# Splitting the up-projection weights of three pairs ahead of time and interleaving their products at the seam between output projection and feed-forward

## The chip, the cores and the metric

The kernel runs on one core of a Trainium2 chip as one launch. The metric is the device time of a run in microseconds (us); three runs of the kernel before are shown, and their median counts. The profile is one further execution, taken by the hardware profiler.

## What is computed

One decoder block in float32: 1024 positions and 16 learned ones, model width 1024, feed-forward width 4096. The part that matters here is the end of the layer, word for word:

```python
mix = jax.nn.sigmoid(g_s5) * y_s5 + jax.nn.sigmoid(g_m) * y_m
h = _layer_norm(ALPHA * h + mix @ w_o[layer], ln1_g[layer], ln1_b[layer])
ff = jnp.square(jax.nn.relu(h @ w_up[layer] + b_up[layer])) @ w_down[layer]
h = _layer_norm(ALPHA * h + ff, ln2_g[layer], ln2_b[layer])
```

Ahead of it stand one combined input projection, a state-space mixer (S5) with a gated linear unit, and a matrix-memory mixer (mLSTM); `mix` joins the two.

## The kernel before

Every product is made in float32 precision from pieces: an operand is split into a high part (`hi`, type float32r, an `activation` Copy on ScalarE, ACT) and a low part (`lo`, the difference, a `tensor_tensor` on VectorE, DVE), and `mm3` (lines 208 to 225) issues three matmuls for each term: hi by hi, hi by lo, lo by hi. TensorE (PE) therefore waits for ACT and DVE wherever an operand has just been split.

The work runs in stages. First the layer norm of the input, then a list of jobs (`ORDER`, then the GLU jobs and the jobs `g`/`m` with `ym`), each of which loads a weight tile, splits it, multiplies and evacuates. Beside the jobs run "lanes": generators that issue a few instructions whenever the matmuls issued so far have moved a notional clock past the time that the generator yielded. One of them, `ah_scale` (line 1090), prepares the residual `ALPHA * h` row by row and stores it in DRAM; it is added when the first GLU job begins.

Then comes the seam that the change is about. `wo_mm` (line 1227) multiplies one of eight rows of 128 positions (t = 0 to 7) by `w_o`: two halves of 512 columns, 24 matmuls each, each evacuated on DVE into `ACC[t]` (line 1233). `ln1_norm` (line 1235) takes the statistics (DVE `bn_stats` on both halves, `bn_aggr`, a square root on ACT, a reciprocal and three Newton steps on DVE) and normalises the row; `ln1_tr` (line 1241) transposes it on PE (8 transposes), scales it on ACT and DVE into `hf`, and splits part of it into `h1h` and `h1l`.

The up product of the feed-forward follows. `w_up` is taken in 16 pairs of column blocks, and each pair is multiplied by a scheme of seven products (numbers 1 to 7, `BLKS`) of 12 matmuls each in place of eight. Products 1, 2 and 3 use `h1h`/`h1l` (`H1`); products 4 to 7 use sums of the row blocks made by `h1_sums` (four DVE instructions for each of four column groups c = 0 to 3) and split by `h1_split` into `th`/`tl` (`T[n]`, one ACT and one DVE instruction for each c). Products 1 and 2 need only the rows t = 0 to 3. Each pair's weights are likewise summed (`up_sums`, four DVE instructions) and split (`split_to`, lines 1305 to 1308, into `wuh`/`wul`) while the pair ahead is multiplied; products of one pair accumulate on each other in PSUM, so that product 2 waits until ACT has copied the result of product 1 out (line 1361), and product 7 until DVE has added product 6 (line 1367).

At the seam the first two pairs are loaded early (`up_load`), products 1 and 2 of pairs 0 and 1 stand around the last transposes, and everything else that they need is summed and split there and then. The order of instructions on each engine is chosen by a scheduler that simulates the program at build time, except inside `tc.manual_schedule`, where the order of the code is kept. All DMAs are issued on SyncE's queue (SP), in order. Tiles come from pools: `slot` has 30 buffers of a row block, `espot` has four, `mmps` has five PSUM banks, `sdps` three.

Of the kernel before, what the change touches and what calls it, by code (L numbers as in the profile page):

```python
# [108 lines left out]
def decoder_block(  # L109
# [18 lines left out]
    def mmps(name="mm"):  # L128
        return psum.tile([P, 512], F32, tag="mm", bufs=5, name=name)
# [959 lines left out]
    def ah_scale():  # L1089
        gb = [slot("gB0"), slot("bB0")]  # L1090
        for i in range(2):
            nc.sync.dma_start(gb[i][:, :D], row_bcast(ln0r, D, i * D))
        rs = {}
        for t in range(9):
            if t < 8:
                rs[t] = slot("ahr")
                nc.sync.dma_start(rs[t][:, :D], ah0_dr[t * P:(t + 1) * P, :])
            if t == 0:
                yield 4.0
                for i in range(2):  # L1100
                    v_.tensor_scalar(gb[i][:, :D], gb[i][:, :D], ALPHA, None, op0=OP.mult)
                yield 2.0
                continue
            r = rs.pop(t - 1)
            for i, op in enumerate((OP.mult, OP.add)):
                v_.tensor_tensor(r[:, :D], r[:, :D], gb[i][:, :D], op=op)
                yield 4.5
            nc.sync.dma_start(ah_dr[(t - 1) * P:t * P, :], r[:, :D])

    for w in ORDER.split():  # L1110
        n, i = w[0], int(w[1:])
# [56 lines left out]
    for i, j in enumerate(jobs):  # L1168
        if j.raw is None and j.w is None:
            load_w(j)  # L1170
        if j.w is None:
            split_w(j)
        if j.ran:
            next_split(jobs, i)
        for d in (1, 2):
            if i + d < len(jobs) and jobs[i + d].raw is None and jobs[i + d].w is None:
                load_w(jobs[i + d])
        if j.tag == S5_START:
            lanes["s5c"].add(s5_pre())
        if j.tag and j.tag[0] == "o":  # L1180
            while int(j.tag[1:]) not in HMREADY:
                lanes["cv"].drain()
                lanes["ml"].step()
        if j.tag == "glu":
            lanes["ah"].add(ah_scale())
        if j.tag == "hmo":
            for l in lanes.values():
                l.drain()
            mid_ctx.close()
            ring_ctx = ExitStack()  # L1190
            ring[0] = ring_ctx.enter_context(tc.tile_pool(name="ring", bufs=1, side="left"))
# [35 lines left out]
    def wo_mm(t):
        hi, lo = MH.pop(t)
        for c0, c1 in HALF:
            ps = mmps()  # L1230
            mm3(ps, [(hi[:, k * P:(k + 1) * P], lo[:, k * P:(k + 1) * P], wo_hi[:, k, c0:c1], wo_lo[:, k, c0:c1])
                     for k in range(KT)])
            v_.tensor_tensor(ACC[t][:, c0:c1], ps, ACC[t][:, c0:c1], op=OP.add)

    def ln1_norm(t):
        acc = ACC[t]
        mv, y = row_stats(acc, "l1", const)
# [54 lines left out]
    def h1_split(n):  # L1292
        T[n] = (f8("th", F32R), f8("tl", F32R))
        for c in range(4):
            r = {1: RAW[c][:, 0:512], 2: RAW[c + 4][:, 512:1024], 3: RAW[c + 4][:, 0:512], 4: RAW[c][:, 512:1024]}[n]
            r = c3(r)
            a_.activation(c4(T[n][0], c * P), r, AF.Copy)
            v_.tensor_tensor(c4(T[n][1], c * P), r, f32(c4(T[n][0], c * P)), op=OP.subtract)  # L1298

    def up_load(p):  # L1300
        UR[p] = [espot("wur"), espot("wur")] if p < 2 else [slot("wur"), slot("wur")]
# [9 lines left out]

    def up_sums(p):
        r1, r2 = UR[p]
        a11, a12, a21, a22 = r1[:, 0:512], r1[:, 512:1024], r2[:, 0:512], r2[:, 512:1024]
        n1, n2 = slot("wus"), slot("wus")
        v_.tensor_tensor(n1[:, 0:512], a21, a22, op=OP.add)
        v_.tensor_tensor(n1[:, 512:1024], n1[:, 0:512], a11, op=OP.subtract)
        v_.tensor_tensor(a21, a11, a21, op=OP.subtract)
        v_.tensor_tensor(n2[:, 0:512], a12, n1[:, 512:1024], op=OP.subtract)
        UR[p] += [n1, n2]  # L1320
# [33 lines left out]
    def up_step(p, n):  # L1354
# [12 lines left out]
            v_.tensor_tensor(c["e2"][:, 0:512], c["b"], c["p1"], op=OP.add)  # L1367
        elif n == 2:
            up_prod(p, 2, c["a"], False)
            c["x1"] = slot("upx")  # L1370
            x = c["x1"][:, 0:512]
# [208 lines left out]
    mix_split(0)  # L1580
    mix_split(1)
    ah_load(0)
    PRE = 2
    for t in range(8):
        if t + 1 < 8:
            ah_load(t + 1)
        wo_mm(t)
        if t == 0:
            for tt in range(2, 8):
                mix_split(tt)  # L1590
            MIX.clear()
        ln1_norm(t)
        if t > 0:
            ln1_tr(t - 1)
        if t > 4:
            h1_sums(t - 5)
        if t in (5, 6):
            up_load(t - 5)
        if t in (6, 7):
            PREP[1](t - 6)  # L1600
    up_step(0, 1)
    ln1_tr(7)
    up_step(0, 2)
    h8_ctx.close()
    ffn[0] = ctx.enter_context(tc.tile_pool(name="ffn", bufs=1, side="right"))
    h1_sums(3)
    h1_split(2)
    up_step(1, 1)
    up_sums(0)
# [9 lines left out]
    for p in range(NP):
        todo = [n for n in UPO if p >= PRE or n not in (1, 2)]  # L1620
        nxt = []
        if p + 1 < NP:
            nxt = [n for n in range(5) if p + 1 >= PRE or n != 1]
        if PRE <= p + 2 < NP:
# [119 lines left out]
```

## Time and profile before

| | us |
|---|---|
| runs of the kernel before | 1574.76, 1576.25, 1576.30 |
| median | 1576.25 |
| the profiled execution | 1577.17 |
| its span, first to last instruction | 1575.1 |
| PE busy in the span | 1531.5 |
| DVE busy | 1020.1 |
| ACT busy | 592.0 |

The time of an execution is the span and some 2 us around it. A line of a timeline gives the start, the duration, the engine, the source line, the operation with the tile that it writes and the tiles that it reads, and in brackets how long the engine had been idle before it and which engine and line released it. Matmuls are pipelined: the duration shown for one is longer than the distance from its start to the next one's start, and it is that distance which counts.

### The profile page before, as it was taken

What the parts mean: (1) busy time and instruction counts of PE and PEld (TensorE: products, weight loads), DVE (VectorE), ACT (ScalarE), POOL (GpSimd) and SP (SyncE); (2) the same over time, 40 slices, a digit from 0 to 9 for tenths busy, and PEclk for the clock granted to TensorE, in tenths of its full rate; (3) what the DMA queues carried; (4) which work ended last, traced back from release to release, by engine and by line L of the source; (5) the groups of instructions that cost most, each with busy time, mean ns of one, the idle gap of its engine ahead of it and who ended that gap; (6) DMA issues with size and microseconds to landing.
All of it is one profiled execution on the core that took longest, in us unless ns stands there. A gap on an engine that the chain in (4) does not pass through costs nothing.

```text
span 1575.1 us, 20280 instructions
## 1 busy us (share of the span) xinstructions
PE 1531.5 (97%) x7679; PEld 1289.3 (82%) x7679; DVE 1020.1 (65%) x1984; ACT 592.0 (38%) x916; POOL 112.0 (7%) x153
## 2 busy tenths in 40 slices
PE   7899999999999999999999989999999999999997
PEld 7898988998777888878888877888888787888886
DVE  7677555489767725632228687566666579875886
ACT  4433253423354332221115244444444434432440
POOL 3200000254214000000000000000000000000000
PEclk9999999999999999999999999999999999999999
DMA  6301212212332443521124204444443699666742
GB/s 233 123 18 56 85 41 98 82 35 78 105 88 67 131 139 126 193 74 52 43 94 161 81 40 138 133 148 147 151 150 132 199 354 374 204 226 232 237 170 107
DMA packets 99010, 210.50 MB, mean 134 GB/s; under 512 B 15240, under 2 KB 33104, under 8 KB 98912
## 3 DMA queue, kind: packets, MB, share of 16 engines
q1 hardware_dynamic: 98912, 209.21, 39.5%
q8 instruction: 60, 0.98, 0.3%
q14 instruction: 38, 0.31, 0.1%
HBM read 153.40 MB, written 54.60 MB: 132 GB/s over the span
## 4 chain that ended last, share of the span: by engine, by line
PE 88%; DVE 7%; ACT 2%; DMA 2%; issue 1%; SPq 0%; POOLq 0%; ACTq 0%; DVEq 0%
PE mm L223 21%; PE mm L222 21%; PE mm L221 21%; PE sd L222 5%; PE sd L223 5%; PE sd L221 5%; PE mm L217 2%; PE pu L474 1%; PE pn L470 1%; PE pn L471 1%; DMA wiB<-wrow_dr 1%; DVE hf L1039 1%; DVE cy L296 1%; DVE tl L1298 1%; PE pt L510 1%
## 5 line engine op out<-in xcount | busy, mean ns | idle before, releaser
L223 PE MATMUL mm<-hT_hi,wlo 128*128 128x512 f32 (+3 forms) x576 | 216.2, 378 | 5.3 <-DVE wlo L203 5.3
L221 PE MATMUL mm<-hT_hi,whi 128*128 128x512 f32 (+3 forms) x576 | 218.4, 379 | 0.3 <-ACT whi L202 0.3
L222 PE MATMUL mm<-hT_lo,whi 128*128 128x512 f32 (+3 forms) x576 | 216.3, 375 | 0.0
L203 DVE TENSOR_TENSOR wlo<-wraw,whi 128x1024 fp32r<-128x1024 f32 (+1 forms) x58 | 71.8, 1240 | 97.1 <-ACT whi L202 96.8
L223 PEld LDWEIGHTS mm<-hT_hi,wlo 128*128 128x128 f32 x576 | 108.5, 189 | 22.5 <-DVE wlo L203 5.8
L221 PEld LDWEIGHTS mm<-hT_hi,whi 128*128 128x128 f32 x576 | 108.7, 189 | 17.1 <-issue 0.5
L222 PEld LDWEIGHTS mm<-hT_lo,whi 128*128 128x128 f32 x576 | 108.7, 189 | 16.7 <-issue 0.2
L1465 ACT ACTIVATE dwh<-wdr 128x1024 fp32r<-128x1024 f32 x56 | 58.9, 1054 | 97.6 <-DVE wdr L1450 32.6
L202 ACT ACTIVATE whi<-wraw 128x1024 fp32r<-128x1024 f32 (+1 forms) x60 | 62.8, 1053 | 84.0 <-PE mm L222 74.0
L222 PE MATMUL sd<-dwl,dah 128*128 128x512 f32 x240 | 94.4, 393 | 0.0
L223 PE MATMUL sd<-dwh,dal 128*128 128x512 f32 x240 | 94.2, 393 | 0.0
L221 PE MATMUL sd<-dwh,dah 128*128 128x512 f32 x240 | 91.9, 393 | 0.0
L1462 DVE TENSOR_TENSOR dal<-da,dah 128x1024 fp32r<-128x1024 f32 x56 | 68.1, 1218 | 33.9 <-ACT dah L1461 32.8
L221 PE MATMUL mm<-dwh,dah 128*128 128x512 f32 (+1 forms) x224 | 84.1, 378 | 1.3 <-ACT dwh L1465 1.3
L222 PE MATMUL mm<-dwl,dah 128*128 128x512 f32 (+1 forms) x224 | 84.6, 379 | 0.4 <-DVE dwl L1466 0.3
L223 PE MATMUL mm<-dwh,dal 128*128 128x512 f32 (+1 forms) x224 | 84.3, 377 | 0.0
L1461 ACT ACTIVATE dah<-da 128x1024 fp32r<-128x1024 f32 x56 | 58.7, 1051 | 63.3 <-DMA da<-act_dr 33.5
L1308 DVE TENSOR_TENSOR wul<-wus,wuh 128x1024 fp32r<-128x1024 f32 (+1 forms) x32 | 30.6, 957 | 74.4 <-issue 58.0
L1573 POOL TENSOR_TENSOR arow<-arow,b2B 128x256 f32<-128x256 f32 x1 | 1.1, 1088 | 1065.0 <-ACT arow L1572 1065.0
L222 PE MATMUL mm<-tl,wuh 128*128 128x512 f32 x192 | 75.9, 395 | 0.9 <-DVE tl L1298 0.9
L221 PE MATMUL mm<-th,wuh 128*128 128x512 f32 x192 | 75.9, 396 | 0.8 <-DVE upe L1367 0.8
L223 PE MATMUL mm<-th,wul 128*128 128x512 f32 x192 | 76.0, 396 | 0.0
(409 smaller groups left out, 3765.4 us busy)
## 6 DMA issues: line engine op xcount, KB each, us to landing
da<-act_dr SPq DMA_DIRECT2D x56, 512.0 KB, 5.7
wdr<-in_wdn_dram SPq DMA_DIRECT2D x56, 512.0 KB, 6.1
wraw<-in_wf_dram SPq DMA_DIRECT2D x36, 512.0 KB, 4.6
wur<-in_wup_dram SPq DMA_DIRECT2D x32, 512.0 KB, 4.3
act_dr<-upy SPq DMA_DIRECT2D x64, 256.0 KB, 3.0
act_dr<-upx SPq DMA_DIRECT2D x48, 256.0 KB, 2.7
wdr<-in_wdn_dram SPq DMA_DIRECT2D x8, 1024.0 KB, 9.9
hm_dr<-hmF SPq DMA_DIRECT2D x8, 512.0 KB, 3.0
```

The lines of the kernel that those rows point to most:

```text
L202: a_.activation(hi[:, :n], r[:, :n], AF.Copy)
L203: todo.append(lambda e=v_, r=r, hi=hi, lo=lo, n=n: e.tensor_tensor(lo[:, :n], r[:, :n], f32(hi[:, :n]), op=OP.subtract))
L217: t_.matmul(ps, tm[i], tm[j], start=(w == 0 and k == 0), stop=(w == 2 and k == n - 1))
L221: t_.matmul(ps, ah, bh, start=(i == 0 and part[0]), stop=False, skip_group_check=skip)
L222: t_.matmul(ps, ah, bl, start=False, stop=False, skip_group_check=skip)
L223: t_.matmul(ps, al, bh, start=False, stop=(i == n - 1 and part[1]), skip_group_check=skip)
L296: v_.scalar_tensor_tensor(y[:, :LEN], pre[:, w:w + LEN], convt[:, ci, w:w + 1], y[:, :LEN], op0=OP.mult, op1=OP.add)
L470: t_.matmul(pn[:, :257], qi[:, c0:c0 + n], Cs[c][:, :257], start=True, stop=False)
L1308: v_.tensor_tensor(lo[:, :n], raw[:, :n], f32(hi[:, :n]), op=OP.subtract)
L1461: a_.activation(ah[:, :D], a[:, :D], AF.Copy)
L1462: v_.tensor_tensor(alo[:, :D], a[:, :D], f32(ah[:, :D]), op=OP.subtract)
L1465: a_.activation(wh, raw[i], AF.Copy)
```

## The change

Four things are done.

1. The weights of the first three pairs (`PRE = 3`) are loaded, summed and split much earlier, by a new generator `up_early` in the lane of `ah_scale`. For each pair it makes the seven weight blocks as hi and lo beside each other in one tile `wpre` and stores the tile to a DRAM buffer `wu_dr` on SP: 21 stores. `ah_scale` now starts at job `g4`, three jobs ahead of the GLU jobs, and yields 1.5 instead of 4.5, and `up_early` follows it.
2. At the seam these 21 tiles are read back from `wu_dr` by `pre_load`: 128 x 1024 elements each, into the four `espot` buffers, issued on GpSimd's queue (POOL), with a float32 source and a float32r destination. Four loads are issued ahead; after that each product issues the load of the product four places behind it, when it has released its own buffer.
3. The 21 products of the three pairs are interleaved: 1 and 2 of all three pairs first, with the transposes of the last row between, then product 6 of the three pairs, product 7 of the three, then 5, 4 and 3. The order on DVE and PE is that of the code from `ln1_norm(5)` up to product 7 of the third pair (`tc.manual_schedule` for these two engines); ACT, SP and POOL keep the scheduler's order. The statistics of a half row are taken right behind its evacuation, and the transposes of rows 5 and 6 stand between the halves of rows 6 and 7.
4. The tile `x1` of a pair is dropped; its two results are written into the halves of `e1`.

The diff, cut to its core:

```diff
@@ up_early, a new generator behind ah_scale (whose yield goes from 4.5 to 1.5)
+    wu_dr = dram.tile([PRE, 7, P, 1024], F32, name="wu_dr")
+    def up_early():
+        for p in range(PRE):
+            r = [slot("wur"), slot("wur")]
+            for j in range(2):
+                nc.sync.dma_start(r[j][:, :D], wup[2 * p + j].rearrange("p k f -> p (k f)"))
+            yield 3.0
+            a11, a12, a21, a22 = r[0][:, 0:512], r[0][:, 512:1024], r[1][:, 0:512], r[1][:, 512:1024]
+            n1, n2 = wsums(a11, a12, a21, a22)
+            yield 3.0
+            for n, w in ((1, a11), (2, a12), (3, n2[:, 0:512]), (4, a22), (5, n1[:, 0:512]), (6, n1[:, 512:1024]),
+                         (7, a21)):
+                o = slot("wpre", F32R)
+                a_.activation(o[:, 0:512], w, AF.Copy)
+                v_.tensor_tensor(o[:, 512:1024], w, f32(o[:, 0:512]), op=OP.subtract)
+                nc.sync.dma_start(wu_dr[p, n - 1], f32(o[:, 0:1024]))
+                yield 0.9
@@ where the lanes are fed
-        if j.tag == "glu":
+        if j.tag == "g4":
             lanes["ah"].add(ah_scale())
+            lanes["ah"].add(up_early())
@@ the loads at the seam
+    def pre_load(p, n):
+        w = espot("wpre", F32R)
+        g_.dma_start(w, wu_dr[p, n - 1])
+        UW[p, BLKS[n][0]] = (w[:, 0:512], w[:, 512:1024])
@@ the seam (before: one loop over the eight rows, then the pairs one by one)
+    todo = [(0, 1), (1, 1), (0, 2), (2, 1), (1, 2), (2, 2)] + [(p, n) for n in (6, 7, 5, 4, 3) for p in range(PRE)]
+    loads = iter(todo)
+    def pre(p, n):
+        up_step(p, n)
+        ld = next(loads, None)
+        if ld:
+            pre_load(*ld)
+    for _ in range(4):
+        pre_load(*next(loads))
+    with tc.manual_schedule(engines={mybir.EngineType.DVE, mybir.EngineType.PE}):
+        ln1_norm(5)
+        wo_row(6, lambda: (ln1_tr(5), h1_sums(0)))
+        ln1_norm(6)
+        h1_sums(1)
+        wo_row(7, lambda: (ln1_tr(6), h1_sums(2)))
+        ln1_norm(7)
+        h8_ctx.close()
+        ffn[0] = ctx.enter_context(tc.tile_pool(name="ffn", bufs=1, side="right"))
+        h1_split(2, range(3))
+        for i in range(6):
+            pre(*todo[i])
+            if i == 2:
+                ln1_tr(7)
+                h1_sums(3)
+                h1_split(2, (3,))
+        h1_split(3)
+        for n, nt in ((6, 1), (7, 4)):
+            for p in range(PRE):
+                pre(p, n)
+                if p == 1:
+                    h1_split(nt, range(2))
+                if p == 2:
+                    h1_split(nt, range(2, 4))
```

What the change does to the order on PE at the seam: before, behind the last matmul of row 7, with what each matmul waits for (`h1h`, `h1l`, `th`, `tl` are the activations, `wuh`, `wul` the weights split at the seam, `ident` marks transposes):

```order
L221 MATMUL mm_8355<-h1h_7733,wuh_8254 128x512 [waits Activation_49]
L223 MATMUL mm_8355<-h1h_7733,wul_8255 128x512 [waits DVE_49]
...
L1252 MATMUL ln1_8325<-ident_74,acc_8052 128x128 [waits DVE_49]
...
L221 MATMUL mm_8427<-h1h_7733,wuh_8351 128x512 [waits Activation_49]
...
L221 MATMUL mm_8355<-h1h_7737,wuh_8254 128x512 [waits Activation_49]
...
L1252 MATMUL ln1_8371<-ident_74,acc_8155 128x128 [waits DVE_49]
...
L221 MATMUL mm_8427<-h1h_7737,wuh_8351 128x512 [waits Activation_49]
...
L222 MATMUL sd_8548<-tl_8479,wuh_8448 128x512 [waits DVE_49]
```

And on PE in the changed kernel, from the first product to the first one that uses the sums (`wpre` are the tiles read back, `DMASW` the semaphores of POOL's loads):

```order
L222 MATMUL mm_8493<-h1h_7848,wpre_8253 128x512 [waits DMASW1_49]
...
L222 MATMUL mm_8476<-h1h_7852,wpre_8255 128x512 [waits DMASW2_49,Activation_49]
...
L1290 MATMUL ln1_8528<-ident_74,acc_8272 128x128 [waits DVE_49]
...
L222 MATMUL mm_8556<-h1h_7848,wpre_8257 128x512 [waits DMASW3_49]
...
L222 MATMUL mm_8493<-h1h_7852,wpre_8491 128x512 [waits DMASW4_49,Activation_49]
...
L222 MATMUL mm_8556<-h1h_7852,wpre_8508 128x512 [waits DMASW5_49,Activation_49]
...
L223 MATMUL mm_8617<-tl_8469,wpre_8525 128x512 [waits DVE_49]
```

The transposes of row 6 have moved ahead of these products (between the halves of row 7), row 7's stand behind three products, no product waits for a weight split on ACT or DVE, and each waits for a load instead.

On DVE, before, from the last evacuation of row 7 on (`L1298` splits `tl`, `L1308` splits weights, `L1233` to `L180` and `L169` to `L172` are row 7's evacuation, statistics and Newton steps, `L1259`, `L1269` and `L1287` to `L1290` belong to row 6):

```order
L1233 TENSOR_TENSOR acc<-mm,acc 128x512
L1298 TENSOR_TENSOR tl<-hf,th 128x4x128
L179 BN_STATS l1st<-acc 128x6
L1298 TENSOR_TENSOR tl<-hf,th 128x4x128 x2
L180 BN_AGGR l1mv<-l1st 128x2
L1298 TENSOR_TENSOR tl<-hf,th 128x4x128 x5
L1259 TENSOR_SCALAR hf<-ln_8325,ln1t 128x128 x2
L1308 TENSOR_TENSOR wul<-wur,wuh 128x1024
L169 RECIPROCAL l1y<-l1y 128x1
...
L170 SCALAR_TENSOR_TENSOR l1u<-l1mv,l1y 128x1
```

And in the changed kernel, from the same evacuation on:

```order
L1264 TENSOR_TENSOR acc<-mm,acc 128x512
L1269 BN_STATS l1st<-acc 128x6
L1274 BN_AGGR l1mv<-l1st 128x2
L170 RECIPROCAL l1y<-l1y 128x1
L171 SCALAR_TENSOR_TENSOR l1u<-l1mv,l1y 128x1
L172 SCALAR_TENSOR_TENSOR l1u<-l1u,l1y 128x1
L173 SCALAR_TENSOR_TENSOR l1y<-l1u,l1y 128x1
L1276 TENSOR_SCALAR acc<-acc,l1mv,l1y 128x1024
L1337 TENSOR_TENSOR tl<-hf,th 128x4x128 x3
```

Row 7's normalisation is now one unbroken run, with the splits of `tl` behind it and no weight split near it.

POOL's queue had no DMA before. In the changed kernel it holds, behind its last work for S5, four loads and then 17 that each wait for PE:

```order
L1346 DMA wpre_8253<-wu_dr_102 128x1024
L1346 DMA wpre_8255<-wu_dr_102 128x1024
L1346 DMA wpre_8257<-wu_dr_102 128x1024
L1346 DMA wpre_8491<-wu_dr_102 128x1024 [waits DMASW0_49,PE_49]
L1346 DMA wpre_8508<-wu_dr_102 128x1024 [waits DMASW1_49,PE_49]
```

What moved here is the delivery of weights: from SP and a split on ACT and DVE to one load on POOL for each product.

## Rows read from the trace of the kernel before

**Rows 1.** The page: its head, and busy time of each engine with its share of the span.

```profile
span 1575.1 us, 20280 instructions
...
PE 1531.5 (97%) x7679; PEld 1289.3 (82%) x7679; DVE 1020.1 (65%) x1984; ACT 592.0 (38%) x916; POOL 112.0 (7%) x153
```

**Rows 2.** Who waited for whom, PE alone, whole span: us in total, times, longest. The first row is the opening layer norm; the other five all lie between 919 and 985 us.

```profile
PE ln L1029 <- DVE x L1022: 11.5, 8, 2.0
PE mm L221 <- ACT wuh L1307: 2.4, 1, 2.4
PE mm L221 <- ACT upe L1361: 2.2, 2, 1.5
PE sd L222 <- DVE tl L1298: 2.1, 1, 2.1
PE mm L222 <- DVE tl L1298: 0.9, 1, 0.9
PE mm L221 <- DVE upe L1367: 0.8, 1, 0.8
```

**Rows 3.** Busy time by stretch at the seam: us of PE, PE weight loads, DVE, ACT and POOL with their instructions in brackets, then the granted PE clock, the DMA share and GB/s.

```profile
925.00:950.00 25.00, 18.43 (x78) 13.82 (x77) 23.02 (x47) 17.23 (x35) 0.00 (x0) 0.93 0.13 53
935.00:940.00 5.00, 5.00 (x18) 3.96 (x17) 5.00 (x14) 2.31 (x4) 0.00 (x0) 0.75 0.00 0
950.00:975.00 25.00, 23.34 (x99) 18.09 (x98) 18.62 (x27) 10.97 (x16) 0.00 (x0) 1.00 0.34 116
```

**Rows 4.** Timeline of PE at the seam, from the first up product on, and two rows out of a steady stretch, 11 matmuls apart.

```profile
926.78 0.40 PE L221 MATMUL mm<-h1h,wuh 128*128 128x512 f32 x1
...
929.55 1.03 PE L1252 MATMUL ln<-ident,acc 128*128 128x128 f32 x8
932.95 0.50 PE L221 MATMUL mm<-h1h,wuh 128*128 128x512 f32 x1 [2.36 <-ACT wuh L1307]
...
935.75 0.63 PE L221 MATMUL mm<-h1h,wuh 128*128 128x512 f32 x1
936.18 0.63 PE L222 MATMUL mm<-h1l,wuh 128*128 128x512 f32 x1
...
943.58 0.50 PE L221 MATMUL mm<-h1h,wuh 128*128 128x512 f32 x1 [1.53 <-ACT upe L1361]
...
949.12 0.50 PE L222 MATMUL sd<-tl,wuh 128*128 128x512 f32 x1 [2.06 <-DVE tl L1298]
...
953.12 0.50 PE L222 MATMUL mm<-tl,wuh 128*128 128x512 f32 x1 [0.88 <-DVE tl L1298]
...
956.74 0.50 PE L221 MATMUL mm<-th,wuh 128*128 128x512 f32 x1 [0.78 <-DVE upe L1367]
...
997.35 0.39 PE L222 MATMUL mm<-tl,wuh 128*128 128x512 f32 x1
...
999.91 0.39 PE L221 MATMUL mm<-th,wuh 128*128 128x512 f32 x1
```

**Rows 5.** Timeline of DVE and ACT: row 7's evacuation, the end of its statistics, its square root, reciprocal and normalisation.

```profile
926.98 0.69 DVE L1233 TENSOR_TENSOR acc<-mm,acc 128x512 f32<-128x512 f32 x1 [2.19 <-PE mm L223]
...
930.05 0.20 DVE L180 BATCH_NORM_AGGREGATE l1mv<-l1st 128x2 f32<-128x12 f32 x1
...
932.79 0.29 ACT L168 ACTIVATE l1y<-l1mv,eps_t 128x1 f32<-128x1 f32 x1
...
934.91 0.15 DVE L169 RECIPROCAL l1y<-l1y 128x1 f32<-128x1 f32 x1
...
940.09 0.81 DVE L1238 TENSOR_SCALAR acc<-acc,l1mv,l1y 128x1024 f32<-128x1024 f32 x1
```

**Rows 6.** Busy time by stretch, columns as in rows 3: from the first up product to the end of PE's last wait.

```profile
926.70:957.00 30.30, 22.07 (x91) 16.11 (x90) 28.27 (x54) 19.97 (x39) 0.00 (x0) 0.94 0.20 72
```

**Rows 7.** Groups of instructions by line and shape: the splits of up weights. Busy us, mean ns of one, idle time before.

```profile
L1308 DVE TENSOR_TENSOR wul<-wur,wuh 128x1024 fp32r<-128x1024 f32 x32 | 38.9, 1215 | 0.8 <-ACT wuh L1307 0.8
...
L1308 DVE TENSOR_TENSOR wul<-wus,wuh 128x512 fp32r<-128x512 f32 x16 | 11.0, 690 | 71.5 <-issue 58.0 <-PE mm L222 11.2 <-PE sd L222 2.3
...
L1307 ACT ACTIVATE wuh<-wus 128x512 fp32r<-128x512 f32 x16 | 10.1, 631 | 24.9 <-DVE wul L1308 24.9
```

**Rows 8.** Busy time by stretch, columns as in rows 3: the GLU jobs.

```profile
575.00:600.00 25.00, 25.00 (x109) 20.27 (x108) 14.63 (x17) 7.08 (x9) 0.00 (x0) 1.00 0.32 112
600.00:625.00 25.00, 25.00 (x109) 20.26 (x108) 12.35 (x15) 5.84 (x8) 0.00 (x0) 1.00 0.48 166
625.00:650.00 25.00, 25.00 (x111) 20.30 (x109) 14.69 (x16) 4.89 (x7) 0.00 (x0) 1.00 0.37 131
650.00:675.00 25.00, 25.00 (x109) 20.27 (x108) 16.03 (x18) 9.09 (x11) 0.00 (x0) 1.00 0.69 235
```

**Rows 9.** DMA issues by line: count, KB each, median us from issue to landing. All of them stand on SP's queue.

```profile
wur<-in_wup_dram SPq DMA_DIRECT2D x32, 512.0 KB, 4.3
...
wdr<-in_wdn_dram SPq DMA_DIRECT2D x8, 1024.0 KB, 9.9
...
ah_dr<-ahr SPq DMA_DIRECT2D x8, 512.0 KB, 3.0
...
arow<-res_dr SPq DMA_DIRECT2D x8, 512.0 KB, 11.8
```

More of the change, by code (lines that the diff above doesn't have):

```diff
@@ L43 @@
 NM = 1
+PRE = 3
 ZD = 1
@@ L1106, in ah_scale, with wsums @@
                 v_.tensor_tensor(r[:, :D], r[:, :D], gb[i][:, :D], op=op)
-                yield 4.5
+                yield 1.5
             nc.sync.dma_start(ah_dr[(t - 1) * P:t * P, :], r[:, :D])
+    wu_dr = dram.tile([PRE, 7, P, 1024], F32, name="wu_dr")
+    def wsums(a11, a12, a21, a22):
+        n1, n2 = slot("wus"), slot("wus")
+        v_.tensor_tensor(n1[:, 0:512], a21, a22, op=OP.add)
+        v_.tensor_tensor(n1[:, 512:1024], n1[:, 0:512], a11, op=OP.subtract)
+        v_.tensor_tensor(a21, a11, a21, op=OP.subtract)
+        v_.tensor_tensor(n2[:, 0:512], a12, n1[:, 512:1024], op=OP.subtract)
+        return n1, n2
+    def up_early():
[14 more added lines that the diff above has]
+                yield 0.9
     for w in ORDER.split():
@@ L1225, in ah_load, with wo_mm @@
         nc.sync.dma_start(ACC[t][:, :D], ah_dr[t * P:(t + 1) * P, :])
[L1227 to L1233, printed above, removed]
+    L1 = {}
+    def wo_mm(t, i):
+        hi, lo = MH[t]
+        c0, c1 = HALF[i]
+        ps = mmps()
+        mm3(ps, [(hi[:, k * P:(k + 1) * P], lo[:, k * P:(k + 1) * P], wo_hi[:, k, c0:c1], wo_lo[:, k, c0:c1])
+                 for k in range(KT)])
+        v_.tensor_tensor(ACC[t][:, c0:c1], ps, ACC[t][:, c0:c1], op=OP.add)
+        if i == 0:
+            L1[t] = const.tile([P, 2, 6], F32, tag="ln_st", bufs=3, name="l1st")
+        else:
+            MH.pop(t)
+        v_.bn_stats(L1[t][:, i, :], ACC[t][:, c0:c1])
     def ln1_norm(t):
         acc = ACC[t]
-        mv, y = row_stats(acc, "l1", const)
+        mv = const.tile([P, 2], F32, tag="ln_mv", bufs=4, name="l1mv")
+        v_.bn_aggr(mv, L1.pop(t).rearrange("p a b -> p (a b)"))
+        y = rsqrt(mv[:, 1:2], 1, "l1", const)
         v_.tensor_scalar(acc[:, :D], acc[:, :D], mv[:, 0:1], y, op0=OP.subtract, op1=OP.mult)
@@ L1290, in h1_sums, with h1_split @@
         v_.tensor_tensor(b21, b21, b22, op=OP.subtract)
-    def h1_split(n):
-        T[n] = (f8("th", F32R), f8("tl", F32R))
-        for c in range(4):
+    def h1_split(n, cs=range(4)):
+        if n not in T:
+            T[n] = (f8("th", F32R), f8("tl", F32R))
+        for c in cs:
             r = {1: RAW[c][:, 0:512], 2: RAW[c + 4][:, 512:1024], 3: RAW[c + 4][:, 0:512], 4: RAW[c][:, 512:1024]}[n]
@@ L1313, in up_sums @@
         r1, r2 = UR[p]
[L1314 to L1320, printed above, removed]
+        UR[p] += list(wsums(r1[:, 0:512], r1[:, 512:1024], r2[:, 0:512], r2[:, 512:1024]))
     PREP = {
@@ L1582, in decoder_block, with wo_row @@
     ah_load(0)
-    PRE = 2
-    for t in range(8):
+    def wo_row(t, between=None):
         if t + 1 < 8:
             ah_load(t + 1)
-        wo_mm(t)
+        wo_mm(t, 0)
+        if between:
+            between()
+        wo_mm(t, 1)
+    for t in range(6):
+        wo_row(t)
         if t == 0:
@@ L1591, in decoder_block @@
             MIX.clear()
-        ln1_norm(t)
+        if t < 5:
+            ln1_norm(t)
         if t > 0:
             ln1_tr(t - 1)
[L1595 to L1609, printed above, removed]
@@ L1617, in decoder_block @@
+    RAW.clear()
+    up_load(PRE)
+    for i, (p, n) in enumerate(todo[-9:]):
+        pre(p, n)
+        if i == 3:
+            up_load(PRE + 1)
+        if i > 3:
+            PREP[i - 4](PRE)
     UPO = (1, 6, 2, 7, 5, 4, 3)
     seq = [(s, n) for n in DNO for s in range(4)]
[L1619 to L1624, printed above, removed]
+    for p in range(PRE, NP):
+        nxt = range(5) if p + 1 < NP else ()
+        if p + 2 < NP:
@@ L1625, in decoder_block @@
             up_load(p + 2)
-        for i, n in enumerate(todo):
+        for i, n in enumerate(UPO):
             up_step(p, n)
```

17 lines of the change are left out of this document (4 added, 13 removed).

## The prediction

> **What bounds the kernel now.** I read the head of the page first: PE is busy for 1531.5 of 1575.1 us [rows 1], so a change can win only what PE does not use, 43.6 us, and can lose whenever it makes PE wait. The list of who waited for whom, for PE alone, says where the idle time lies [rows 2]: 11.5 us are the opening layer norm, which the change does not touch; five waits of 2.4 + 2.2 + 2.1 + 0.9 + 0.8 = 8.4 us lie at the seam, and the rest is scattered. The windows show what the waits have in common: at 925 to 950 DVE is busy for 23.02 of 25 us, ACT for 17.23, and PE falls to 18.43 [rows 3]. Across the whole stretch from the first up product to the end of the last wait DVE is busy for 28.27 of 30.3 us [rows 6]. Here, and nowhere else near, DVE sets the pace.
>
> What does the seam cost? PE's timeline gives it by counting [rows 4]. From 926.78 to 956.74 the program has six products of 12 matmuls and 16 transposes. In the steady stretch 11 matmuls take 999.91 - 997.35 = 2.56 us, so one takes 0.2327 us and a product 2.79; 8 transposes take 1.03. The work is 72 x 0.2327 + 2 x 1.03 = 18.8 us, and the stretch lasts 29.96. **The excess is 11.2 us.** About 8 of it are idle times in brackets (the five waits, without repeats of a group). Much of the rest is the clock: at 935 to 940 PE is fully busy at a mean granted clock of 0.75 [rows 3], a mixture of the 2.4 and the 1.2 GHz level, and two matmuls there start 0.43 us apart instead of 0.2327 [rows 4]; eight such cost 1.6 us. It fell behind the idle times, and it is 1.00 again in 950 to 975. So 11.2 us is the most that this seam can give.
>
> **The change part by part. (a) Removed at the seam.** The waits for `wuh` go, since no product of pairs 0 to 2 waits for a weight split. DVE loses some three splits of 1024 elements (1.215 us each), one of 512 (0.69) and about four weight sums of a like size, 7 us in all; ACT loses about 4.8 us, at 0.63 for 512 [rows 7]. That is what the waits for `tl` and `upe` stand behind: 28.27 of 30.3 us becomes 21.
>
> **(b) Row 7's chain.** Before, from the last evacuation (926.98) to the end of the normalisation (940.90) it takes 13.9 us, of which its own instructions are a few: 0.69 evacuation, 0.20, 0.29, 0.15, 0.81 [rows 5]; the rest is other work scheduled between. Now DVE's order has nothing between: 0.69 + 0.69 statistics + 0.20, the square root on ACT behind one copy of a product, reciprocal and three steps 0.8, normalisation 0.81, semaphores between: about 5.2 us. PE has three products ahead of the transposes, 8.4 us. Slack 3 us.
>
> **(c) From the transposes to product 6.** DVE needs two scalings, two splits, four sums and a `tl`, some 5.7 us at the rates of rows 5 and 7; PE has three products, 8.4 us. ACT's split of the last `th` stands behind an evacuation, so I count the slack as about 1 us, the tightest in the seam. The transposes of rows 5 and 6 stand one half (24 matmuls, 5.6 us) behind their row, for a chain of about 3.7.
>
> **(d) Moved to the GLU stage.** 21 splits on ACT (0.63) and DVE (0.69) and 12 sums of 0.69 [rows 7]: 13.2 us of ACT and 22.8 of DVE. In 575 to 675 PE is busy for all of its 100 us, DVE for 57.7 and ACT for 26.9 [rows 8], so they become about 80 and 40 (less, since `ah_scale` starts earlier): covered. What they could delay is the split of a GLU weight: at worst some eight DVE instructions stand ahead of it, 5.5 us, beside a job of 48 matmuls, 11.2 us. On SP, 21 stores of 512 KB go past the GLU loads. Each waits for its split, and the loads behind it wait with it; a store of this size lands in 3.0 us [rows 9], and the loads lead by about 10. Priced at nothing; if the cover is gone, some of 2 to 6 us return.
>
> **(e) The loads.** Each product waits for a 512 KB load on POOL's queue. There are four buffers, so the load that is issued when a product ends has three products, 8.4 us, to land; with a landing time L the period of a product is the larger of 2.79 and (L + 2.79)/4. **The threshold is L = 8.4 us.** No row shows a load on POOL. The nearest is `wur`, 512 KB on SP in 4.3 us: no stall. The far ends are the 1024 KB load, 9.9 us (period 3.17, 17 loads x 0.38 = 6.5 us lost), and `arow`, 11.8 (3.65, 17 x 0.86 = 14.6 us lost) [rows 9]. Both of these have a reason that is absent here, twice the bytes or a full queue, and the DMA share of the seam is 0.13 to 0.34 [rows 3], so I take 4.3. Below nothing there is no gain, as a load cannot be better than in time.
>
> On this term the Trainium skill ("DMA: Bandwidth & Descriptors", Anatomy of one DMA — SWDGE (gpsimd) path) gives a fit for GpSimd's queue, 2.0 us plus bytes over 436e3; for 524288 bytes that is an estimate of 3.2 us, below the threshold, and the sum would be the same. No run here shows it yet. A rule that speaks against the change is in "SBUF — State Buffer" (Who interferes with whom): GpSimd cannot write its DMAs' descriptors while DVE runs an instruction that holds the port pair they share.
>
> The trace has a candidate for such an instruction: the normalisation handles 1024 elements in 0.81 us [rows 5], where a two-input split of that size takes 1.215 [rows 7]. If loads were held only by it, one load would be up to 0.81 us late, against a slack of 8.4 - 4.3 = 4.1.
>
> **(f) End of the seam.** Products 5, 4 and 3 of three pairs close together, so their additions, relu and squares bunch on DVE: about 16.4 us of it in 17 us of PE. I count 0.9 us for this and for first matmuls behind the fixed places.
>
> **The sum** is made against the profiled execution, 1577.17: 1577.17 - 11.2 + 0.9 = 1566.9. It lies 0.92 above the median of the runs, 1576.25, so I forecast **1566.0 us**.
>
> **The rivals.** *A, the forecast:* the seam's excess goes and little returns, 1563.8 to 1568. The lower end is the whole 11.2 and a little of the scattered waits beside the seam (1576.25 - 11.2 - 1.2).
>
> *B, part given back:* the GLU stage or the bunch at the end costs PE 2 to 6 us more. For it: DVE at 16.4 of 17 in (f), and SP's stores in front of GLU loads. Against: DVE's 12 to 16 of 25 in the GLU stage [rows 8]. 1568 to 1573.
>
> *C, the waits move:* with a fixed order, one DVE instruction that waits for ACT holds all behind it. If row 7's chain stayed at 13.9 us, its transposes would wait 13.9 - 8.4 = 5.5 us; if those of rows 5 and 6 took 7.9 instead of 3.7, they would wait 2.3 each; with one more for the clock that falls behind idle time the sum is 11, all that was won. The time stays at 1573 to 1579.4. Against: only ACT's own work lies between the chain's steps, and it has lost 4.8 us. This is also the case that the change does not do what it says, as the seam would still wait for activations.
>
> *D, slower:* the loads are late. From L = 8.4 us every product waits for its weights; the gain is used up when 17 x ((L + 2.79)/4 - 2.79) = 11.2 us, at L = 11.0. At `arow`'s 11.8 the seam loses 14.6, the sum is 1576.25 - 11.2 + 14.6 = 1579.7, and waits at a low clock add to it. For it: one row does land in 11.8 [rows 9], and no row shows POOL's queue. Against: 4.3 for the same size, 3.0 for stores.
>
> The rule on the shared ports ("SBUF — State Buffer", above, the Trainium skill) is a way in which D could come about: held by every DVE instruction, and not just by the normalisation, a load would wait for gaps in a DVE that is busy for some 21 of 30 us. That the trace has no such load to show leaves D its chance.
>
> **How the numbers follow.** A has 0.62, B 0.17, C 0.09, D 0.12. About 0.2%, or 3.15 us, is what a measurement of this kernel can tell from no change; A and B are faster by more (0.79), C is the same (0.09), D slower (0.12). The likeliest is A, 1566.0. The range must leave out no more than 0.2: C and D together are 0.21, so I take A and B whole and a margin into C, 1563.5 to 1574.0.
>
> **What would show it.** In the changed kernel's list of waits PE should not wait at the seam for `wuh`, `tl` or `upe`, and the granted clock there should be 1.00 throughout; this is (a) to (c). The loads `wpre` should land in 3 to 5 us on POOL's queue, and PE should not wait for a DMA; above 8.4 it is D. PE should stay at 25.00 of 25 through the GLU stage while DVE gains some 23 us there (d); a PE wait for a GLU weight would be B. A wait of PE for the transposes of rows 5, 6 or 7, or for the first `tl`, would be C. The prediction is wrong outright if the counted excess of 11.2 us was not idle time of the program but is needed again elsewhere, or if loads on POOL's queue behave unlike those of SP's.

## The result, and the profile after

| | us |
|---|---|
| runs of the changed kernel (5) | 1560.86, 1561.69, 1561.85, 1563.17, 1563.28 |
| median | 1561.85 |
| kernel before (5 runs), median | 1576.25 |
| ratio, with 95% interval | 0.9913 [0.9899, 0.9927] |
| the profiled execution of the changed kernel | 1560.86 |

The kernel became 14.4 us faster. The forecast was 1566.0 us, 10.25 us faster, with a range from 1563.5; the measured time lies 1.65 us below its lower end. The direction was right, and the gain is 4.2 us larger than the sum gave.

The head of the page of the changed kernel, beside [rows 1]:

```profile
span 1559.1 us, 20457 instructions
...
PE 1526.0 (98%) x7679; PEld 1288.5 (83%) x7679; DVE 1021.3 (66%) x1993; ACT 593.9 (38%) x925; POOL 123.1 (8%) x174
```

PE and DVE do as much as before (7679 matmuls; DVE 1021.3 against 1020.1 us); what went is PE's idle time and its slow matmuls. The next rows show who waited for whom, for PE, in us in total, times, longest; they answer to [rows 2]:

```profile
PE ln L1030 <- DVE x L1023: 11.4, 8, 2.0
PE mm L224 <- DVE wlo L204: 5.2, 2, 3.5
PE pu L475 <- ACT kw L458: 2.5, 1, 2.5
...
PE mm L222 <- ACT whi L203: 0.2, 1, 0.2
```

No row names `wuh`, `tl`, `upe` or `wpre`. Busy time by stretch (columns as in [rows 3]): three at the seam, one where the down projection starts.

```profile
920.00:945.00 25.00, 25.00 (x115) 20.35 (x114) 18.90 (x39) 15.72 (x34) 3.17 (x6) 1.00 0.48 149
945.00:970.00 25.00, 25.00 (x108) 20.13 (x107) 11.80 (x18) 5.79 (x10) 4.75 (x9) 1.00 0.84 257
970.00:995.00 25.00, 25.00 (x108) 20.16 (x108) 18.60 (x27) 13.30 (x20) 1.06 (x2) 1.00 0.80 260
1225.00:1250.00 25.00, 25.00 (x110) 20.34 (x109) 18.62 (x20) 16.72 (x22) 0.00 (x0) 1.00 0.96 321
```

PE is busy for the whole of each stretch at a granted clock of 1.00. Row 7's chain, on DVE and ACT, and PE's transposes behind it, beside [rows 5]:

```profile
926.35 0.68 DVE L1264 TENSOR_TENSOR acc<-mm,acc 128x512 f32<-128x512 f32 x1
927.07 0.69 DVE L1269 BATCH_NORM_STATS2 l1st<-acc 128x6 f32<-128x512 f32 x1
927.80 0.21 DVE L1274 BATCH_NORM_AGGREGATE l1mv<-l1st 128x2 f32<-128x12 f32 x1
...
929.04 0.28 ACT L169 ACTIVATE l1y<-l1mv,eps_t 128x1 f32<-128x1 f32 x1
...
930.14 0.81 DVE L1276 TENSOR_SCALAR acc<-acc,l1mv,l1y 128x1024 f32<-128x1024 f32 x1
...
933.90 1.03 PE L1290 MATMUL ln<-ident,acc 128*128 128x128 f32 x8
```

From 926.35 to 930.95 the chain takes 4.6 us in place of 13.9, and it is ready 2.95 us before PE comes to the transposes at 933.90.

**Where the 14.4 us came from.** On PE's timeline I add up, over a stretch, each distance from one matmul's start to the next less 0.2327 us for each matmul ([rows 4]), and leave out gaps where the record of a matmul is missing from the trace. Around the seam (170 us from the first output-projection matmul on) that loss is 12.3 us before and 0.8 after; the 0.8 are first matmuls behind transposes, 0.08 to 0.09 us each. That is one place. The second one, which I had not priced, is 290 us later, where the up product ends and the down projection begins. PE's list of waits before has a row for it, which [rows 2] does not show, and PE's timeline shows the place:

```profile
PE mm L221 <- ACT dwh L1465: 1.3, 1, 1.3
```

```profile
1248.43 1.19 PE L221 MATMUL mm<-dwh,dah 128*128 128x512 f32 x4 [1.29 <-ACT dwh L1465]
1249.69 0.50 PE L222 MATMUL mm<-dwl,dah 128*128 128x512 f32 x1
...
1300.30 0.50 PE L222 MATMUL mm<-dwl,dah 128*128 128x512 f32 x1 [0.34 <-DVE dwl L1466]
```

The losses there sum to 2.5 us: 1.46 and 0.50 around the two waits, and 0.33, 0.10 and 0.11 in matmuls behind them that start late. After, this loss is 0.0. The reason stands in SP's queue. These are its stores of activations and its first loads of the down projection before (start, time in the queue):

```profile
1226.99 11.67 SPq L1352 DMA_DIRECT2D act_dr<-upx  x3
1238.78 0.86 SPq L1434 DMA_DIRECT2D da<-act_dr  x2
1240.04 0.90 SPq L1427 DMA_DIRECT2D wdr<-in_wdn_dram  x2
```

And after, up to PE's first matmul of the down projection:

```profile
1218.67 0.32 SPq L1390 DMA_DIRECT2D act_dr<-upx  x1
1219.09 0.88 SPq L1471 DMA_DIRECT2D da<-act_dr  x2
1220.06 0.90 SPq L1464 DMA_DIRECT2D wdr<-in_wdn_dram  x2
1226.18 0.34 SPq L1390 DMA_DIRECT2D act_dr<-upx  x1
...
1233.35 0.40 PE L222 MATMUL mm<-dwh,dah 128*128 128x512 f32 x1
```

Before, three stores of `upx` stand ahead of the loads and the last of them waits until 1238.6 for ACT; the loads are issued 9.65 us ahead of the first product. After, a store stands behind the loads, and they have 14.26 us. The two places give 11.5 + 2.5 = 14.0 us of the 14.4. The two profiled executions are further apart, 16.3 us (1577.17 and 1560.86): 14.0 of these lie behind the first output-projection matmul (at 832.21 and 830.23), and 1.9 ahead of the first `pu` matmul (at 154.29 and 152.42), where no edit reaches. That part is a difference between executions and not the change's.

### The profile page after: what moved, and what is told of

The parts are those of the page before. It is cut to its first block, busy times and chain, and to the rows that moved or that the text cites. A ratio compares the mean times of both kernels' runs of the same rounds, so it can differ in the third digit from the quotient of the medians.

```text
span 1559.1 us, 20457 instructions
## 1 busy us (share of the span) xinstructions
PE 1526.0 (98%) x7679; PEld 1288.5 (83%) x7679; DVE 1021.3 (66%) x1993; ACT 593.9 (38%) x925; POOL 123.1 (8%) x174
## 4 chain that ended last, share of the span: by engine, by line
PE 76%; issue 16%; DVE 5%; ACT 1%; DMA 1%; POOLq 0%; SPq 0%; ACTq 0%; DVEq 0%
PE mm L224 20%; PE mm L222 20%; PE mm L223 20%; PE sd L222 2%; PE sd L223 2%; PE sd L224 2%; PE mm L218 2%; PE pu L475 1%; PE pn L471 1%; PE pn L472 1%; DMA wiB<-wrow_dr 1%; DVE hf L1040 1%; DVE cy L297 1%; PE pt L511 0%; DVE u L1014 0%
## 5 line engine op out<-in xcount | busy, mean ns | idle before, releaser
L222 PE MATMUL mm<-whi,hT_hi 128*128 128x256 f32 (+1 forms) x256 | 75.4, 294 | 0.5 <-DVE mlo L347 0.5
L1503 DVE TENSOR_TENSOR dwl<-wdr,dwh 128x1024 fp32r<-128x1024 f32 x56 | 68.2, 1219 | 11.6 <-ACT dwh L1502 11.1
L224 PE MATMUL mm<-whi,hT_lo 128*128 128x256 f32 (+1 forms) x256 | 74.2, 290 | 0.0
L223 PE MATMUL mm<-wlo,hT_hi 128*128 128x256 f32 (+1 forms) x256 | 73.8, 288 | 0.0
L224 PE MATMUL mm<-th,wul 128*128 128x512 f32 x156 | 61.6, 395 | 0.0
```

The source lines that it names most:

```text
L222: t_.matmul(ps, ah, bh, start=(i == 0 and part[0]), stop=False, skip_group_check=skip)
L223: t_.matmul(ps, ah, bl, start=False, stop=False, skip_group_check=skip)
L224: t_.matmul(ps, al, bh, start=False, stop=(i == n - 1 and part[1]), skip_group_check=skip)
L1503: v_.tensor_tensor(wl, raw[i], f32(wh), op=OP.subtract)
```

## The experiments

The seam and down-start columns are the loss as above, from each kernel's profile; ratios are to the kernel before on the same chip (medians there 1576.24 for e1 to e4, 1577.38 for e5 to e8, 1576.62 for e9 to e12).

| kernel | median us | ratio [95%] | seam | down start |
|---|---|---|---|---|
| before | 1576.25 | | 12.3 | 2.5 |
| changed | 1561.85 | 0.9913 [0.9899, 0.9927] | 0.8 | 0.0 |
| e1 `x1` dropped alone | 1576.67 | 1.0001 [0.9992, 1.001] | 16.7 | 0.0 |
| e2 changed, `x1` kept | 1562.5 | 0.9909 [0.9895, 0.9923] | 0.8 | 1.7 |
| e3 early work alone | 1574.42 | 0.9987 [0.9978, 0.9996] | 12.3 | 1.7 |
| e4 order alone, fixed | 1584.11 | 1.0044 [1.003, 1.0058] | 21.4 | 2.1 |
| e5 loads asked for earlier | 1573.98 | 0.9981 [0.997, 0.9992] | 12.5 | 0.0 |
| e6 pre-split alone | 1580.71 | 1.002 [1.0011, 1.0029] | 15.7 | 2.8 |
| e7 changed, order free | 1567.62 | 0.9938 [0.9925, 0.9952] | 6.2 | 0.0 |
| e8 two loads asked ahead | 1560.27 | 0.989 [0.9877, 0.9904] | 0.8 | 0.0 |
| e9 two buffers | 1580.23 | 1.0026 [1.0017, 1.0036] | 15.6 | 0.0 |
| e10 two pairs | 1570.12 | 0.9953 [0.9941, 0.9966] | 6.9 | 0.0 |
| e11 loads on SP | 1562.36 | 0.9904 [0.9891, 0.9918] | 0.8 | 0.0 |
| e12 order alone, free | 1582.26 | 1.0033 [1.0021, 1.0046] | 19.6 | 2.5 |

**The second place: e1, e2, e5.** e1 takes part 4 into the kernel before.

```diff
-            c["x1"] = slot("upx")
-            x = c["x1"][:, 0:512]
+            x = c["e1"][:, 512:1024]
...
```

> The kernel before with part 4 alone: x1 dropped, its results in the halves of e1. Theory 1 (the 3 to 4 us beyond the forecast come from the start of the down projection: one buffer less per pair lets the scheduler put the first loads da and wdr one store earlier on SP): the PE wait for dwh (1.3 us) and the slow matmuls behind it go, the seam keeps its five waits, time 1573 to 1574. Rival (the whole gain is at the seam and part 4 does nothing by itself): 1576.2.

The waits at the start of the down projection went, as theory 1 said, but the time did not move: the seam lost 4.4 us more. (By the trace e1 should then be 1.9 us slower; the runs show 0.2, with an interval of -1.3 to 1.6, and the profiled execution took 1578.51, above the median of 1576.67.) The timeline of e1 shows how; ACT, then DVE:

```profile
939.48 0.69 ACT L1371 ACTIVATE upe<-mm,bupt 128x512 f32<-128x512 f32 x1 [2.88 <-PE mm L223]
940.06 0.62 ACT L1297 ACTIVATE th<-hf 128x512 fp32r<-128x512 f32 x1
```

```profile
940.71 0.69 DVE L1298 TENSOR_TENSOR tl<-hf,th 128x512 fp32r<-128x512 f32 x1 [2.09 <-ACT th L1297]
...
941.92 0.81 DVE L1238 TENSOR_SCALAR acc<-acc,l1mv,l1y 128x1024 f32<-128x1024 f32 x1
```

The scheduler put a relu that waits for PE ahead of a split of `th` on ACT; DVE waited for the split, and row 7's normalisation stood behind that. Rival C has this mechanism, a DVE instruction that waits for ACT and holds what is behind it; here it comes about in the scheduler's order, where C looked for it in a fixed one. e2 is the same edit undone in the changed kernel.

> The changed kernel with part 4 alone undone: x1 is a tile of its own again. Theory 1: the PE wait for dwh at the start of the down projection comes back, seam without waits, time 1564 to 1565.5. Rival: no wait comes back, 1561.9.

SP's queue and PE's first product of the down projection in e2:

```profile
1213.53 11.66 SPq L1390 DMA_DIRECT2D act_dr<-upx  x3
1225.28 0.88 SPq L1472 DMA_DIRECT2D da<-act_dr  x2
...
1234.04 1.19 PE L222 MATMUL mm<-dwh,dah 128*128 128x512 f32 x4 [0.39 <-ACT dwh L1503]
```

The three stores stand ahead of the loads again. The wait for `dwh` came back (0.4 us, and 0.4 for `dwl`), 1.7 us of loss in all, where the kernel before had 2.5; e3, the kernel before with the early work, has 1.7 too. The time, 1562.5, can't be told from 1561.85: the trace shows this loss, the runs do not resolve it. e5 leaves the seam alone and moves only the loads in the kernel before:

```diff
-                if i == 1:
+                if i == 0:
                     dn_fetch(*seq[0])
```

> The kernel before with one number changed at the far end of the up product: the first loads of the down projection (da, wdr) are asked for one step earlier, so that they stand two stores further ahead on SP; everything up to there, the seam too, is as before. Theory 1 (the start of the down projection is a second place, worth some 2.5 us, and e1 lost at the seam what it won there): waits for dwh and dwl gone, the seam's five waits unchanged, 1573 to 1574. Rival (what PE wins there is given back later): 1576.2.

The ratio of 0.9981 is 3.0 us, its interval 1.3 to 4.7; the loss at the down start went from 2.5 to 0.0 and the seam's is as before (12.5). What PE wins there is kept. That the order of loads against stores on SP costs this time is shown; that dropping `x1` is what changed that order in the change is shown by e1 and e2 together, whose only edit it is. The other profiles agree. In all six with `x1` in which the loads are asked for as before, 101 stores of activations stand ahead of the first load, it is issued 8.6 to 9.7 us ahead of its product, and the loss is 1.7 to 2.8 us. In all seven without `x1` it is 100 stores, 14.3 us and no loss; in e5, 99 stores, 18.0 us and no loss.

**The early work: e3.** The generator `up_early` and the earlier `ah_scale` are put into the kernel before, and nobody reads the stored tiles.

> The kernel before with the early work alone: the 21 tiles are summed, split and stored in the GLU stage as in the changed kernel, and nobody reads them; the seam is that of before. Theory 1 (early work is fully covered by PE): 1576.2, no wait of PE for a GLU weight, DVE busy some 23 us more. Rival (it costs PE time in the GLU stage, and the seam gains more than 11): 1578 to 1582.

The seam's loss is that of before, and PE is busy for 25.00 of 25 us in each of the four GLU stretches. Of the changed kernel the same stretches show, beside [rows 8]:

```profile
575.00:600.00 25.00, 25.00 (x109) 20.26 (x109) 17.47 (x19) 9.59 (x11) 0.00 (x0) 1.00 0.56 196
600.00:625.00 25.00, 25.00 (x109) 20.28 (x109) 15.46 (x22) 9.88 (x17) 0.00 (x0) 1.00 0.68 255
...
650.00:675.00 25.00, 25.00 (x109) 20.24 (x108) 15.89 (x21) 10.35 (x15) 0.00 (x0) 1.00 0.87 334
```

By the ratio e3 is 2.0 us faster (0.6 to 3.5), where no change was expected; 0.8 of it is the down start, and for the rest no place was found. The early work costs PE nothing that shows.

**Splits and order: e4, e12, e6, e7, e10.** e4 and e12 take the new order of rows, transposes and products, for the two pairs of the kernel before, with all weights still split at the seam; e4 fixes the order on DVE and PE, e12 leaves it to the scheduler.

```diff
+    with tc.manual_schedule(engines={mybir.EngineType.DVE, mybir.EngineType.PE}):
+        ln1_norm(5)
+        wo_row(6, lambda: (ln1_tr(5), h1_sums(0)))
+        ln1_norm(6)
+        PREP[1](0)
+        h1_sums(1)
+        wo_row(7, lambda: (ln1_tr(6), h1_sums(2)))
+        ln1_norm(7)
+        PREP[1](1)
...
```

> The kernel before with part 3 alone, for the two pairs that it has: fixed order on DVE and PE, transposes of rows 5 and 6 between the halves, statistics behind each half, products 1 and 2 of the two pairs interleaved; all weights are still split at the seam. Theory 1 (DVE and ACT have some 7 us too much to do at the seam, the order alone can't remove it): waits of 4 us or more stay at the seam, 1569 to 1576. Rival (the order is what matters, the pre-split weights are not needed): 1564 to 1566.

> As e4 (all weights split at the seam, rows, transposes and products in the changed order, two pairs), with the fixed order taken off DVE and PE. If e4 was slow because its hand order put weight splits badly: 1574 to 1578, waits at the seam 8 to 12 us as before. If this order of rows and products is itself worse while weights are split there: 1580 to 1585.

PE's waits in e4:

```profile
PE mm L222 <- ACT wuh L1326: 7.0, 2, 6.6
PE mm L224 <- DVE wul L1327: 6.2, 1, 6.2
```

and in e12:

```profile
PE sd L222 <- ACT th L1316: 5.8, 1, 5.8
...
PE mm L222 <- ACT wuh L1326: 2.4, 1, 2.4
```

With weights split at the seam the new order is worse than the old, fixed or not: the theory's 1569 to 1576 for e4 was too good, and that I fixed the order by hand is not the main reason, since e12 is hardly better (1582.26). e6 is the opposite half: weights of two pairs split early and read back, the old order of the code, the scheduler's order.

> Parts 1 and 2 without part 3, for two pairs: weights split early, stored and read back on POOL, 14 loads, but the code's order of the rows, transposes and products is that of before and the scheduler sets the order. Theory 1 (the splits are most of the seam's loss): no wait for wuh, waits at the seam of 2 to 5 us in all for the transposes and sums, 1566 to 1571. Rival (without the order the pre-split weights win little): 1572 to 1576.

This was a miss in sign: 1580.71, slower than before. The waits of PE, and DVE's rows of row 7:

```profile
PE ln L1280 <- DVE acc L1266: 4.0, 1, 4.0
PE mm L221 <- DMA wpre<-wu_dr: 3.6, 2, 3.3
...
PE mm L221 <- ACT upe L1394: 1.1, 1, 1.1
```

```profile
927.12 0.69 DVE L1261 TENSOR_TENSOR acc<-mm,acc 128x512 f32<-128x512 f32 x1 [2.91 <-PE mm L223]
...
939.70 0.81 DVE L1266 TENSOR_SCALAR acc<-acc,l1mv,l1y 128x1024 f32<-128x1024 f32 x1
```

Without one weight split near it, row 7's chain still takes 13.4 us, since the scheduler fills it with splits of `tl`, sums and scalings. And PE waited 3.3 us for a load, which was issued at 958.04, only 2.98 us ahead of its product. My reading is that the loads keep the code's order while the scheduler moved the products; no run tests it. e7 takes only the fixed order off the changed kernel.

> The changed kernel with the fixed order on DVE and PE taken off; the code is in the same order, and the scheduler may move instructions. Theory 1 (the scheduler does as well once the splits are gone): 1561 to 1564, waits at the seam under 1.5 us. Rival (the fixed order carries part of the gain): 1566 to 1571, waits for the transposes or the first tl.

It gives back 4 us of the gain by the ratios and 5.4 by the trace: waits of 2.3 us for `th` and 1.1 for `upe`, and matmuls 0.43 us apart behind the first of these. Row 7's chain is at 13.4 us again (924.66 to 938.06), with splits of `tl`, sums and scalings between its steps. The rival holds. e10 takes two pairs in place of three.

> The changed kernel with two pairs in place of three (PRE = 2, 14 tiles, four products around the last transposes in place of six, two ahead of them). Step (b): two products give 5.6 us for a chain of 4.6 us, step (c): two products behind the transposes give 5.6 us for about 5.7 us of DVE work and ACT's splits behind it: wait of 0.5 to 2.5 us for th or tl, 1562.5 to 1565.5. Rival (two pairs are enough): 1560 to 1562.

The wait for `th` is 2.0 us, as expected, but the loss is 6.1 us more than with three pairs: behind that wait the granted clock is 0.73 at 945 to 950, and 1.6 us are a wait for a load `wpre` after the fixed stretch. The third pair's two products are the cover. e10 is also what e4 and e6 are to be compared with, as all three have two pairs: the seam's loss is 12.3 us before, 15.7 with the early splits alone, 21.4 with the order alone, and 6.9 with both (e10, which also has `x1` dropped). Neither half was run alone with three pairs.

**The loads: e8, e9, e11.** e8 asks for two loads ahead in place of four.

> The changed kernel with two loads ahead in place of four. Theory (e): two products in L + 2.79 us; with the 4.8 us that a load took in the changed kernel the period is 3.8 us, 1.0 us lost on each of 19 loads, 1581; with 4.0 us, as fewer loads share the DMA engines, 3.4 us and 1573. PE waits for wpre. Rival (loads on POOL are served at once and faster than their landing times say): under 1565.

This told nothing of the term: the buffers, four as before, are what a load waits for, so all loads but the last started where they did. It serves as a second set of runs of the same order: 1560.27 beside 1561.85. e9 gives the loads two buffers of their own.

```diff
-        return ext.tile([P, D], dt, tag="e", bufs=4, name=name)
+        return ext.tile([P, D], dt, tag="e", bufs=2, name=name)
...
-        w = espot("wpre", F32R)
+        w = ext.tile([P, D], F32R, tag="w", bufs=2, name="wpre")
...
```

> The changed kernel with two buffers for the loads wpre in place of four (the other two stay for upy), so that a load can start only when the product two places ahead of its own has ended. Term (e): two products in L + 2.79 us; with a landing of 4.0 to 4.8 us the period is 3.4 to 3.8 us in place of 2.79, 19 loads lose 0.6 to 1.0 us each, 11 to 19 us in all: 1573 to 1581, PE waits for DMA wpre. Rival (a load has landed well before its landing time says): under 1566.

PE's waits, and three first matmuls with the load between them (PE, then POOL):

```profile
PE mm L222 <- DMA wpre<-wu_dr: 8.1, 9, 2.2
...
PE sd L222 <- DMA wpre<-wu_dr: 3.4, 3, 1.3
...
PE mm L222 <- ACT wuh L1351: 1.1, 2, 0.9
```

```profile
963.04 0.47 PE L222 MATMUL mm<-th,wpre 128*128 128x512 f32 x1 [1.34 <-DMA wpre<-wu_dr]
...
970.18 0.47 PE L222 MATMUL sd<-th,wpre 128*128 128x512 f32 x1 [1.28 <-DMA wpre<-wu_dr]
...
977.33 0.50 PE L222 MATMUL sd<-th,wpre 128*128 128x512 f32 x1 [1.21 <-DMA wpre<-wu_dr]
```

```profile
966.39 0.53 POOL L1346 DMA_DIRECT2D wpre<-wu_dr  x1 [3.86 <-PE mm L224]
```

Two products take 7.15 us. The load starts 0.56 us behind the point at which a product of 2.79 us would have ended (963.04 + 2.79 = 965.83), and 3.79 us later the product at 970.18 begins. So two products take L + 0.56 + 2.79. If all 19 loads went like this they would lose 19 x (7.15/2 - 2.79) = 14.9 us; the 12 waits for `wpre`, with the slow matmuls behind them, cost 14.7 in the trace, unevenly. The medians of e9 and the changed kernel are 18.4 us apart. Of these 17.0 lie between the first matmul of the output projection and the first of the down projection (420.08 us against 403.12); the column for the seam ends ahead of the last 2.4 of them, and 1.8 are waits for `wuh` and `wul` with the slow matmuls behind them. The rest was not followed; two buffers for `upy` are part of the edit.

e11 issues the loads on SP.

> The changed kernel with the 21 loads on SP's queue in place of POOL's, where they stand in order with the stores of the activations. Theory (a load behind a store that waits for ACT or DVE is late): PE waits for wpre of 1 to 5 us, 1563 to 1568. Rival (the four buffers cover that too): 1560 to 1562.

PE did not wait: with four buffers the queue does not matter here. The median landing was 4.4 us on SP; on POOL it was 4.3 in e8 and, in the changed kernel, 4.8:

```profile
wpre<-wu_dr POOLq DMA_DIRECT2D x21, 512.0 KB, 4.8
```

## Why the prediction came out as it did

- **The bound at the seam was right.** The prediction named 11.2 us of excess; 12.3 - 0.8 = 11.5 us went, in a stretch that is a little longer. No idle time and no low clock stayed.
- **The sum failed at an edit without a price.** "The change part by part" ends at the seam; part 4, the dropped tile `x1`, has no term, and the waits outside of the seam were put down as "the rest is scattered". Two of them, for `dwh` and `dwl`, stood at the start of the down projection (1.29 and 0.34 us in the rows above) and cost 2.5 us with the matmuls around them. e5 shows that the place is worth this, e1 and e2 that part 4 reorders SP there; in the changed kernel 1.7 of the 2.5 us come back without part 4 (e2), and 0.8 are away with the early work as well (e3). The forecast was 4.15 us too high: 2.5 are this place, 0.9 are (f), 0.3 the seam, and 0.45 are less than the five runs differ by. The lower end of the range had (f) at nothing and 1.2 us for scattered waits, so what puts the time below it is the rest of this place, 1.3 us, and 0.3 at the seam. Run times alone do not show it: the interval of the ratio is 4.4 us wide, and e2, with `x1` kept, lies below the range as well (1562.5).
- **(f) was mis-sized.** The 0.9 us for the bunch at the end of the seam did not come: PE is busy for 25.00 of 25 at 970 to 995 with DVE at 18.60. The DVE work was counted rightly, but 17 us is not the PE time beside it: products 5, 4 and 3 of three pairs are nine, 9 x 2.79 = 25.1 us, and with matmuls of the fourth pair between they lie from 959.99 to 988.00, where DVE is busy for 16.53 of 28.01 us. With terms of -11.5, 0.0 and -2.5 the sum is 1577.17 - 14.0 - 0.92 = 1562.25, beside 1561.85.
- **(a) was half right.** It says that weight splits are what the waits for `tl` and `upe` stand behind. e6 took them away and the seam lost more. Splitting early is needed for the gain (without it e4 and e12 lose 21.4 and 19.6), and so is the order (e6: 15.7); the last 5 us need the order to be fixed (e7).
- **(b) and (c) held.** The chain was put at 5.2 us and took 4.6, and its slack was 2.95 us against 3. PE did not wait for `tl`: the one that product 6 needs was written by 942.5 and first read at 943.36, a slack of 0.9 us against about 1. With two pairs this cover is too short, and PE waits 2.0 us for `th` (e10).
- **(d) held.** PE lost nothing in the GLU stage. DVE was put at 80 of 100 us; it is 65.4 (17.47 + 15.46 + 16.53 + 15.89), since `ah_scale` moved ahead (the last of its instructions starts at 595.5 in place of 662.8).
- **(e) held, with a term missing.** The median landing of 4.8 us lies under 8.4. e9 shows the formula with 0.56 us more for each load, so the threshold for L is 7.8. The last three loads of the changed kernel took 8.0, 8.9 and 8.0 us, above it, and PE did not wait: their products begin behind 11 matmuls of the fourth pair, which the scheduler put ahead of them (976.85 to 979.41). So the median alone does not show that the loads were in time.
- **The rivals.** B's bunch and C's waits did not come in the changed kernel. C's waits came in e1 and e7, where the order is the scheduler's; the fixed order, which C blames, is what took the chain from 13.4 us (e7) to 4.6. What late loads cost is shown by e9, which is slower than the kernel before (ratio 1.0026). The Trainium skill ("DMA: Bandwidth & Descriptors", Anatomy of one DMA — SWDGE (gpsimd) path) gave an estimate of 3.2 us; it was too low here, as the loads took 4.8, and 3.8 in e9. Of the Trainium skill's port rule ("SBUF — State Buffer", Who interferes with whom) nothing is seen: POOL's single issues last 0.53 or 0.54 us throughout, with DVE's splits beside them. A normalisation lies beside an issue once, in e7, for 0.12 us (937.26 to 937.38), and both take their usual time, 0.80 and 0.53 us; that is too little to test the rule.

## What to carry to other kernels

Price every edit of a diff, the small one too: a tile less changes what a scheduler may place where, and its effect can lie hundreds of microseconds from the edit. With two pairs, pre-splitting weights and the new order each made the seam slower alone (by 3.4 and 9.1 us) and faster together (by 5.4 us); so try such edits as a pair before dropping either. A queue that carries stores in order holds the loads behind them; look there when an engine waits at the start of a stage for something that was free to load long before.

## What the runs showed of the hardware

- Idle time did not always bring a lower clock. In e9 PE was busy for 23.31 of 30 us at 940 to 970, in waits of 0.5 to 2.2 us, at a granted clock of 1.00; before, behind a wait of 2.4 us, it fell to 0.75 in a stretch [rows 3], and in e10, behind one of 2.0 us, to 0.73 at 945 to 950.
- POOL's issue of a load starts 0.30 us behind the end that the profile gives for the last matmul that it waits for (e9: 966.09 and 966.39), and the issue itself holds POOL for 0.53; on SP (e11) the distance is 0.03 us (929.93 and 929.96).
- Stretches that no edit touches differ between executions: from the first `pu` matmul to the first of the output projection 677.8 us in the changed kernel and 676.4 in e8, which runs the same order; the first `pu` matmul itself starts between 151.80 and 154.29 us in the fourteen profiles. A difference of a microsecond or two needs its place in the trace, not the total alone.
